# Order of the value projections and of the last products in the second mixer's head pairs

## The chip, the cores and the metric

The kernel runs on one core of a Trainium2 chip. The metric is the device time of one execution in microseconds. The kernel before took 2727.28 us (median of 3 runs, 2727.0 to 2727.28).

## The reference

One step of an encoder with two layers, 1024 channels, over a prompt of 1024 frames and 8 running streams of 16 frames each (1152 rows in all). Layer 0 mixes with stick-breaking attention and a convolution; layer 1, the one that the change touches, with attention in a band of chunks. After each mixer comes a residual and an MLP. The mixer of layer 1:

```
def c_project(h, w_in):
    p = (h @ w_in).reshape(B, T, 3, N_C_HEADS, HEAD_DIM)
    return p[:, :, 0], p[:, :, 1], p[:, :, 2]
...
def band_attention(q, k, v, q_pos, k_pos, rel_bias):
    s = jnp.einsum('bqhd,bkhd->bhqk', q, k).astype(jnp.float32) * (HEAD_DIM ** -0.5)
    rel = jnp.clip(q_pos[:, None] - k_pos[None, :], -REL_CLIP, REL_CLIP) + REL_CLIP
    s = s + rel_bias[:, rel].astype(jnp.float32)
    ...
    p = jax.nn.softmax(jnp.where(mask, s, -jnp.inf), axis=-1)
    return jnp.einsum('bhqk,bkhd->bqhd', p.astype(v.dtype), v)
...
o = lax.map(one_chunk, jnp.arange(T // CHUNK))
return o @ w_out, k[:, T - keep:], v[:, T - keep:]
```

It has 16 heads of 64 channels; a frame sees its chunk of 64 and the 8 chunks before. The new keys and values are outputs too.

## The kernel before

Channels lie on the 128 partitions and frames along the free axis, in three groups of 384. Every float32 operand of a matmul is split into a high and a low part (`split`: ACT copies the high part, L185, DVE subtracts it, L186), and each product is made of three matmuls.

The program is written as lists of steps. `Step(pe, go, dve, name, after, lag)` holds an estimated TensorE time, the code that issues the instructions, and optionally a name, and the name of a step that has to end some time (`lag`, ns) ahead. `merge` takes several such lists and makes one: of the heads that are ready on an estimated TensorE clock, it takes the one of the list that is least far along. `run` issues them. A scheduler then lays down each engine's queue; what an engine issues, it issues in that order.

The second mixer (`mixer1`) works on head pairs p = 0 to 7. A pair's work:

- **Projections.** Chunk 3p + n is q (n = 0), k (n = 1) or v (n = 2) of pair p: 72 matmuls `psc<-h,hl_wc` of 128 x 384, 24 for each of the three groups. A chunk's weights come in two halves `hl_wc{chunk}_0` and `_1`, loaded by SP into one of three staging buffers and split by ACT and DVE into one of four buffers; so the halves of a chunk go where those of the chunk two before it were. `staged` multiplies the sums by the row's norm (DVE, L1141) into `sq`, `sk` or `sv` and stores keys and values (POOL's DMA queue).
- **`expand_qk`.** For each of the two heads i, ACT copies k (L348) and q (L350), DVE makes the low parts l (L351) and q (L353), each 64 x 1024, and DMAs copy k and l to the other partitions.
- **`expand_v`.** TensorE turns the values (`vt`, L1169), and they are split into `vs`.
- **Jobs (i, t).** i is the head, t a quarter of the frames; each has two blocks q = 2t and 2t + 1 of 128 rows. `one(q)`: scores `zc` (L1220, L1221), bias and minimum on DVE (L1184, tile `s{p}{i}{q}`), exponential on ACT (L1187), reciprocal and scaling on DVE (L1188, L1189). Then `split_weigh_steps`: transposes of the weights in two or three groups gi (`tpc{p}{i}{t}{gi}`, L457), their parts `whc` (ACT) and `wlc` (DVE), the products `avc{p}{i}{t}` (L469), `atc` (ACT, L477), `cpc` (DVE, L479), and a DMA to `cat_d`. A job's transposes and products (its tail) are carried and woven into the next job by `pipeline`, and those of a pair's last job into the next pair.
- **Sample.** The running streams' attention of the pair (`zs`, `zn`, `st`, `so`, `sq`) is merged in.

All of this is merged per pair. Before the change, the fill of pair p was the three chunks of pair p + 1 (`proj(p + 1)`), with those of pair 0 issued ahead of the loop; the list of the pair's steps began with the carried ones, and `bias_p` and `expand_qk` were called just ahead of the merge.

Pair 7 has no pair to project for. Its fill is the output projection (`part_out`: `psoa<-cat,hl_wo1a`, added to `xo`, which is loaded from `x_d`, L1100, L1105), whose input `cat` comes from the pairs before: `ready_chunks` loads a pair's result (`cr<-cat_d`, L1081) and splits it into `cat`. `cr` uses the buffer of `sk`, `xo` those of `sq` and `sv`.

Of the kernel before, what the change touches and what calls it, by code (L numbers as in the profile page):

```python
# [22 lines left out]
NG = 3  # L23
# [29 lines left out]
def merge(*lists):  # L53


    lists = [steps for steps in lists if steps]
    total = [sum(s.pe for s in steps) or 1.0 for steps in lists]
    at, done = [0] * len(lists), [0.0] * len(lists)
    out, now = [], 0.0
    ends = {s.name: 1e9 for steps in lists for s in steps if s.name}  # L60
    while True:
        heads = []
        for n, steps in enumerate(lists):
            if at[n] < len(steps):
                s = steps[at[n]]
                ready = max(now, ends.get(s.after, -1e9) + s.lag)
                heads.append((ready, (done[n] + 0.5 * s.pe) / total[n], n, s))
        if not heads:
            return out
        now, _, n, s = min(heads, key=lambda e: e[:3])  # L70
        out.append(s)
        at[n] += 1
        done[n] += s.pe
        now += s.pe
        if s.name:
            ends[s.name] = now
# [22 lines left out]
def run(steps):  # L99
    for s in steps:  # L100
        s.go()
# [23 lines left out]
def tile_trunk(ctx, tc, ins, outs):  # L125
# [17 lines left out]
    def bank(name):  # L143
        return psum.tile([P, 512], F32, tag="ps", name=name)
# [165 lines left out]
    def chunk_steps(n, got, ahead, h, ks, evac, name, depth=1, per=12):  # L310

        steps = [Step(0.0, lambda: [ahead(n + d) for d in range(depth + 1)], 1200.0)]
        for g in range(NG):
            box = {}

            def ps(g=g, box=box):
                if "p" not in box:
                    box["p"] = bank(f"ps{name}{g}")
                return box["p"]

            steps += dense(ps, lambda: got[n], h, g, ks, per)
            steps.append(Step(0.0, lambda g=g, ps=ps: evac(ps(), g), 470.0))
        return steps

    def chunks_steps(ns, got, ahead, h, ks, evac, name, depth=1):

        steps = [Step(0.0, lambda: [ahead(n) for n in range(ns[0], ns[-1] + depth + 1)])]
        for g in range(NG):
            for n in ns:
                box = {}  # L330

                def ps(g=g, n=n, box=box):
                    if "p" not in box:
                        box["p"] = bank(f"ps{name}{n}{g}")
                    return box["p"]

                steps += dense(ps, lambda n=n: got[n], h, g, ks)
                steps.append(Step(0.0, lambda n=n, g=g, ps=ps: evac(n, ps(), g), 470.0))
        return steps
# [303 lines left out]

        return cs

    def pipeline(jobs, carry):


        steps = []
        for first, second, tail in jobs:  # L650
            h = (len(carry) + 1) // 2
            steps += [first] + carry[:h] + [second] + carry[h:]
            carry = tail
        return steps, carry

# [419 lines left out]
    def ready_chunks(layer, chunks, pp, cat_t):  # L1075

        steps = []
        for c in chunks:
            def go(c=c):
                cr = pp.tile([P, T], F32, "sk", f"cr{layer}{c}")  # L1080
                dma(cr, cat_d[layer][c])  # L1081
                for g in range(NG):
                    hi, lo = (x[:, c % 4, :] for x in cat_t[g][c // 4])
                    split(hi, lo, cr[:, g * G:g * G + G])
            steps.append(Step(300.0, go))
        return steps
# [29 lines left out]
    def mixer1(nx, win):  # L1116
        h, rstd = nx.h, nx.r
        with ExitStack() as st:
            ep = Bufs(st.enter_context(pool("early1")), s=4, bp=2)
            cp = Bufs(st.enter_context(pool("cache1")), ct=2)  # L1120
            pp = Bufs(st.enter_context(pool("pair1")))
# [6 lines left out]
            got, ahead = win  # L1128
            ks = range(KC)

            def staged(p, n, ps, g):
                tag = ("sq", "sk", "sv")[n]
                if p == 0 and n < 2:
                    if n == 0:
                        nx.run_rows(g)
                    elif g == 0:
                        nx.end(1)
                        nx.end(2)
                if g == 0:
                    S[tag, p] = pp.tile([P, T], F32, tag, f"{tag}1{p}")  # L1140
                tt(S[tag, p][:, g * G:g * G + G], ps[:, :G], rstd[g], ALU.mult)  # L1141
                if g == 2 and n:
                    put(outs["c_k" if n == 1 else "c_v"][p], S[tag, p])

            def proj(p):
                if p == 0:
                    return (chunks_steps([0, 1], got, ahead, h, ks, lambda n, ps, g: staged(0, n, ps, g), "c")
                            + [Step(0.0, lambda: expand_qk(0))]
                            + chunk_steps(2, got, ahead, h, ks, lambda ps, g: staged(0, 2, ps, g), "c02"))
                steps = []  # L1150
                for n in range(3):
                    steps += chunk_steps(3 * p + n, got, ahead, h, ks, lambda ps, g, n=n: staged(p, n, ps, g),
                                         f"c{p}{n}")
                return steps

            def expand_qk(p):
                q, k = S["sq", p], S["sk", p]
                expand(qs, kd, kl, q, k)
                S["qn"] = pp.tile([P, P], F32, "qn", f"qn1{p}")
                S["kn"] = pp.tile([P, P], F32, "kn", f"kn1{p}")  # L1160
                ACT(S["qn"], q[:, TP:], AF.Copy, scale=0.125)
                ACT(S["kn"], k[:, TP:], AF.Copy)

            def expand_v(p, g):
                v = S["sv", p]
                tp = bank(f"vt1{p}{g}")
                for i in range(3):
                    c = (3 * g + i) * P
                    nc.tensor.transpose(tp[:, i * P:(i + 1) * P], v[:, c:c + P], ident)  # L1169
                n = 3 if g < 2 else 2  # L1170
                tv = tp[:, :G].rearrange("p (j h d) -> p j h d", j=3, h=2)
                dst = vs[:, 3 * g:3 * g + n]
                split(dst[:, :, :, 0, :], dst[:, :, :, 1, :], tv[:, :n])
                if g == 2:
                    S["vn"] = pp.tile([P, P], F32, "vn", f"vn1{p}")
                    ACT(S["vn"], tp[:, 2 * P:3 * P], AF.Copy)
# [22 lines left out]
            def bias_p(p, i):  # L1199
                bp = ep.tile([P, 640], F32, "bp", f"bp{p}{i}")  # L1200
                dma(bp, ins["bias_p"][2 * p + i])
                nc.gpsimd.memset(bp[0:64, 576:640], NEG)
                nc.gpsimd.memset(bp[64:128, 0:64], NEG)
                S["bp", p, i] = bp
# [34 lines left out]
            def soft(bg, z, zn, s):  # L1239
# [3 lines left out]
                softmax(w, [(z[0], bs[:, 0:512], 0, 512), (zn[:, 0:P], bs[:, c:c + P], 512, P)], 640, f"s{p}{bg}")  # L1243
                s["w"] = w

            run(proj(0))
            carry, cat_t = [], None
            for p in range(8):
                S["p"] = p
                if p == 7:  # L1250
                    cat_t = new_hs("cat1")
                cat = Cat(1, p, wk, cat_t)
                jobs = attend(p, cat)
                s3 = jobs[3][0]
                s3.go = lambda p=p, go=s3.go: (bias_p(p, 1), go())
                body, left = pipeline(jobs[1:], jobs[0][2])
                steps = carry + [jobs[0][0]]
                steps += [Step(327.0, lambda p=p, g=g: expand_v(p, g)) for g in range(NG)]
                if p == 7:
                    bias_p(p, 0)  # L1260
                    expand_qk(p)
                    run(merge(steps, ready_chunks(1, range(3), pp, cat_t)))
                    steps = []
                steps += [jobs[0][1]] + body
                carry = left
                cs = sample_out(cat, wk, p)
                sample = [Step(0.0, lambda p=p: biases(p))]
                load = sample_caches(1, p, cp)
                sample += two_samples(*(sample_steps(1, p, bg, S, wk, load, soft, cs) for bg in range(2)))
                back = []  # L1270
                if p < 7:
                    fill = proj(p + 1)
                else:
                    fill = sum(part_out(1, range(3), pp, cat_t), [])
                    steps += carry
                    back = ready_chunks(1, range(3, 7), pp, cat_t)
                if p < 7:
                    bias_p(p, 0)
                    if p:
                        expand_qk(p)  # L1280
                run(merge(steps, sample, fill, back))
            return cat_t

# [527 lines left out]
    with pool("mlp0") as mp_:  # L1811
# [3 lines left out]
        early = []  # L1815
# [170 lines left out]
```

## Time and profile before

| | |
|---|---|
| median of 3 runs | 2727.28 us |
| profiled execution, its own time | 2730.68 us |
| its span in the trace | 2728.9 us |
| mean TensorE clock granted | 0.993 |
| second mixer's pair 3, from the sq of pair 2's end to that of its own | 70.2 us |
| window from the end of pair 6 to the end of pair 7's merge | 89.6 us |

So 1.8 us of the profiled execution lie around the span, and it took 3.4 us more than the median. In the page of the profile a group of instructions has a line, an engine, out<-in by the program's names, shapes and a count, then the busy time and the mean of one, then the idle time ahead of them and what ended most of it. In a timeline each row is a stretch of equal instructions with its start, length, and in brackets the idle ahead of it with its releaser. The largest groups of the second mixer's projections read:

```
L225 PE MATMUL psc<-h,hl_wc 128*128 128x384 f32 x1728 | 327.1, 339 | 0.0
L225 PEld LDWEIGHTS psc<-h,hl_wc 128*128 128x128 f32 x1728 | 296.8, 188 | 13.3 <-issue 10.9
```

### The profile page before, as it was taken

The numbers are of one execution on the slowest core, as the hardware profiler recorded it, in microseconds if no ns is written. First come the engines' busy times: TensorE is split into PE (matmuls) and PEld (weight loads), VectorE is DVE, ScalarE is ACT, GpSimd is POOL, SyncE is SP. The second block draws the span as 40 slices with busy tenths as digits, with TensorE's granted clock in tenths as the row PEclk, the third lists the DMA queues.
The fourth block names the chain that finished last, engine by engine and source line by source line (L and its number), as shares of the span: only waits on it lengthen the run. The fifth ranks groups of instructions, "written<-read, shape, count | busy, mean of one in ns | idle before, by whom it ended". The sixth has DMA issues, their size and how long they took to land.

```text
span 2728.9 us, 50505 instructions
## 1 busy us (share of the span) xinstructions
PE 2662.6 (98%) x19362; PEld 2553.8 (94%) x19362; DVE 2040.6 (75%) x4105; ACT 1365.7 (50%) x2854; POOL 330.5 (12%) x599
## 2 busy tenths in 40 slices
PE   8999998999999999999999999998999999999998
PEld 8888886899999999999999999997999999999998
DVE  7999996787777755768577777778787777647577
ACT  5344456755555543445355555555455555534344
POOL 1000111131111100000011111110321111100001
PEclk9999999999999999999999999999999999999999
DMA  4344447443333486335444444446543334674344
GB/s 159 104 128 149 146 141 241 171 145 141 140 138 138 151 290 224 108 113 178 145 141 139 129 139 141 137 127 218 181 140 138 143 141 147 233 254 135 96 125 146
DMA packets 173203, 422.90 MB, mean 155 GB/s; under 512 B 25968, under 2 KB 53808, under 8 KB 170912
## 3 DMA queue, kind: packets, MB, share of 16 engines
q1 hardware_dynamic: 135696, 288.38, 32.6%
q0 software_dynamic: 37120, 131.27, 13.9%
q8 instruction: 152, 2.49, 0.4%
q14 instruction: 91, 0.75, 0.1%
q10 hardware_dynamic: 144, 0.02, 0.0%
HBM read 289.60 MB, written 117.34 MB: 149 GB/s over the span
## 4 chain that ended last, share of the span: by engine, by line
PE 84%; DVE 7%; ACT 3%; issue 3%; DMA 3%; POOL 0%; SPq 0%; DVEq 0%; ACTq 0%; POOLq 0%
PE pd L1705 26%; PE um L1480 25%; PE psc L225 10%; PE psp L225 4%; PE avc L469 2%; PE tpc L457 2%; PE psoa L225 2%; PE f L225 1%; PE zs L570 1%; PE zc L1220 1%; PE ava L398 1%; DVE y L737 1%; PE so L604 1%; PE psg L225 1%; PE psa L225 1%
## 5 line engine op out<-in xcount | busy, mean ns | idle before, releaser
L225 PE MATMUL psc<-h,hl_wc 128*128 128x384 f32 x1728 | 327.1, 339 | 0.0
L225 PEld LDWEIGHTS psc<-h,hl_wc 128*128 128x128 f32 x1728 | 296.8, 188 | 13.3 <-issue 10.9
L1480 PE MATMUL um<-sl,hl_m 128*128 128x288 f32 x1548 | 240.8, 296 | 0.0
L1480 PEld LDWEIGHTS um<-sl,hl_m 128*128 128x128 f32 x1548 | 218.2, 189 | 0.0
L1705 PE MATMUL pd<-tm,hl_wd 128*128 128x288 f32 x1584 | 214.7, 294 | 0.0
L1705 PEld LDWEIGHTS pd<-tm,hl_wd 128*128 128x128 f32 x1584 | 211.3, 189 | 0.0
L737 DVE SCALAR_TENSOR_TENSOR y<-u,dw,y 128x1024 f32<-128x1024 f32 (+1 forms) x232 | 177.5, 805 | 0.7
L1487 ACT ACTIVATE hdm<-hdm 128x288 f32<-128x288 f32 x192 | 84.7, 442 | 156.4 <-DVE hdm L1486 154.8
L225 PE MATMUL psp<-h,hl_wi 128*128 128x384 f32 x864 | 162.5, 340 | 0.0
L186 DVE TENSOR_TENSOR tm<-xr,tm 128x576 fp32r<-128x576 f32 (+1 forms) x120 | 85.7, 715 | 94.8 <-ACT tm L185 94.6
L225 PEld LDWEIGHTS psp<-h,hl_wi 128*128 128x128 f32 x864 | 148.4, 188 | 6.2 <-issue 5.1
L185 ACT ACTIVATE tm<-xr 128x576 fp32r<-128x576 f32 (+1 forms) x120 | 77.6, 647 | 94.7 <-PE pd L1705 75.9
L1480 PE MATMUL um<-sl,hl 128*128 128x288 f32 x756 | 119.1, 296 | 0.0
L1187 ACT ACTIVATE s<-s,mxc 128x640 f32<-128x640 f32 (+4 forms) x128 | 88.8, 694 | 60.2 <-DVE mxc L1184 58.6
L1705 PE MATMUL pd<-th,hl_wd 128*128 128x288 f32 x792 | 113.9, 297 | 3.8 <-DVE th L186 3.7
L1705 PEld LDWEIGHTS pd<-th,hl_wd 128*128 128x128 f32 x792 | 108.7, 191 | 4.5 <-DVE th L186 4.2
L1705 PE MATMUL pd<-xr,hl_wd 128*128 128x288 f32 x792 | 111.9, 295 | 0.0
L1705 PEld LDWEIGHTS pd<-xr,hl_wd 128*128 128x128 f32 x792 | 107.4, 189 | 0.0
L1480 PEld LDWEIGHTS um<-sl,hl 128*128 128x128 f32 x756 | 106.4, 188 | 0.8
L1705 PE MATMUL pd<-tm,hl 128*128 128x288 f32 x768 | 104.9, 295 | 0.0
L1705 PEld LDWEIGHTS pd<-tm,hl 128*128 128x128 f32 x768 | 103.1, 188 | 0.0
L185 ACT ACTIVATE whc<-tpc 128x512 fp32r<-128x512 f32 (+1 forms) x144 | 72.5, 523 | 46.7 <-PE tpc L457 45.7
(530 smaller groups left out, 6536.8 us busy)
## 6 DMA issues: line engine op xcount, KB each, us to landing
xr<-hb_d SPq DMA_DIRECT2D x208, 288.0 KB, 2.9
xr<-in_w_up_dram SPq DMA_DIRECT2D x64, 512.0 KB, 4.0
hb_d<-hdm POOLq DMA_DIRECT2D x96, 288.0 KB, 2.4
hb_d<-t POOLq DMA_DIRECT2D x96, 288.0 KB, 2.4
wm<-in_w_down_dram SPq DMA_DIRECT2D x64, 256.0 KB, 4.1
st_wd<-in_w_down_dram SPq DMA_DIRECT2D x64, 256.0 KB, 3.5
st_wc<-in_w_in_c_dram SPq DMA_DIRECT2D x44, 256.0 KB, 2.6
xm_d<-xo POOLq DMA_DIRECT2D x16, 576.0 KB, 3.8
```

What stands on the lines that cost most here:

```text
L185: ACT(hi, src, AF.Copy)
L186: return tt(lo, src, f(hi), ALU.subtract)
L225: mm(ps()[:, :G], hl[:, a, at:at + P], act[g][k // 4][b][:, k % 4, :], start=n == 0, stop=n == len(todo) - 1)
L398: mm(st["av"][64 * m:64 * m + 64, o0:o0 + n], vs[:, j, i], st["w"][gi][:, c0:c0 + n], start=gi == 0, stop=gi == last)
L457: nc.tensor.transpose(tp[:, c0 + q * P:c0 + (q + 1) * P], blocks.get(j, tile_q), ident)
L469: mm(st["av"][:, o0:o0 + n], vs[:, j, i].rearrange("p a d -> p (a d)"), src[:, c0:c0 + n], start=st["done"] == 0, stop=st["done"] == nmm - 1)
L570: mm(box["z"][at // 512][own, at % 512:at % 512 + kw], qb[:, own], k[:, b * kw:b * kw + kw], start=True, stop=True)
L737: stt(src if j == CW - 1 else dst, src, wj, dst, ALU.mult, ALU.add)
L1187: ACT(s[:, :n], s[:, :n], AF.Exp, bias=mx, scale=-1.0, accum_out=tot)
L1480: mm(banks[b, n][:, :TQ], w[:, a, c * P:c * P + P], combo(key, c)[:, h, n * TQ:n * TQ + TQ], start=k < 3 and c == 0 and i == 0, stop=c == ...
L1487: ACT(y, y, AF.Relu)
L1705: mm(ps, w[:, a, m * P:m * P + P], b[:, h, (n - ns[0]) * TQ:(n - ns[0]) * TQ + TQ], start=first and s == 0, stop=j == NJ - 1 and s == 2, s ...
```

## The change

Two things are done in another order; no instruction of the program is removed or added. The values of pair p are projected in the merge of pair p itself, ahead of q and k of pair p + 1, and only q and k of pair 0 are issued ahead of the loop. And for pairs 0 to 6 `pipeline` stops ahead of the second half of the tail of the last job but one: that half and the last job's tail are carried to the next pair. `bias_p` and `expand_qk` become a step `x{p}` at the head of the pair's list, ahead of the carried steps; the first scores wait for it with a lag of 6000 ns, the values' transposes (`turned`) for the end of the value projection. In pair 7 the fill is the value projection, then `ready_chunks` of 0 to 2, then the output projection.

```
-    def pipeline(jobs, carry):
+    def pipeline(jobs, carry, over=False):
...
-            steps += [first] + carry[:h] + [second] + carry[h:]
+            steps += [first] + carry[:h] + [second]
+            if over and tail is jobs[-1][2]:
+                return steps, carry[h:] + tail
+            steps += carry[h:]
             carry = tail
...
-            def proj(p):
-                if p == 0:
...
-                for n in range(3):
+            def proj(p, *ns):
+                steps = []
+                for n in ns:
...
+                steps[-1].name = f"p{p}{ns[-1]}"
...
-            run(proj(0))
+            run(chunks_steps([0, 1], got, ahead, h, ks, lambda n, ps, g: staged(0, n, ps, g), "c"))
...
-                body, left = pipeline(jobs[1:], jobs[0][2])
-                steps = carry + [jobs[0][0]]
-                steps += [Step(327.0, lambda p=p, g=g: expand_v(p, g)) for g in range(NG)]
-                if p == 7:
-                    bias_p(p, 0)
-                    expand_qk(p)
-                    run(merge(steps, ready_chunks(1, range(3), pp, cat_t)))
-                    steps = []
-                steps += [jobs[0][1]] + body
+                body, left = pipeline(jobs[1:], jobs[0][2], p < 7)
+                jobs[0][0].after, jobs[0][0].lag = f"x{p}", 6000.0
+                turned = [Step(327.0, lambda p=p, g=g: expand_v(p, g)) for g in range(NG)]
+                turned[0].after, turned[0].lag = f"p{p}2", 1500.0
+                turned[-1].name = f"v{p}"
+                steps = ([Step(0.0, lambda p=p: (bias_p(p, 0), expand_qk(p)), 0.0, f"x{p}")] + carry
+                         + [*jobs[0][:2]] + turned + body)
...
-                back = []
+                sample[1].after, sample[1].lag = f"x{p}", 7000.0
+                fill, back = proj(p, 2), []
                 if p < 7:
-                    fill = proj(p + 1)
+                    fill += proj(p + 1, 0, 1)
                 else:
-                    fill = sum(part_out(1, range(3), pp, cat_t), [])
                     steps += carry
+                    early = ready_chunks(1, range(3), pp, cat_t)
+                    early[-1].name = "early"
+                    parts = sum(part_out(1, range(3), pp, cat_t), [])
+                    parts[0].after, parts[0].lag = f"v{p}", 0.0
+                    parts[1].after, parts[1].lag = "early", 4000.0
+                    fill += early + parts
                     back = ready_chunks(1, range(3, 7), pp, cat_t)
-                if p < 7:
-                    bias_p(p, 0)
-                    if p:
-                        expand_qk(p)
+                    back[0].after = "early"
                 run(merge(steps, sample, fill, back))
```

**The boundary of pairs 2 and 3.** TensorE's queue before, at the end of pair 2 (`psc322` is the third group of pair 3's values; job (1, 2) of pair 2 is `tpc212`, `avc212`):

```order
L1221 MATMUL zc216384_16953<-l1_14071,q1_14067 128x256
L225 MATMUL psc322_16922<-h1_40_13588,hl_wc11_1_16400 128x384
...
L225 MATMUL psc322_16922<-h1_70_13702,hl_wc11_1_16400 128x384
L457 MATMUL tpc2120_16976<-ident_69,s214_16874 128x128
L457 MATMUL tpc2120_16976<-ident_69,s215_16906 128x128
...
L612 MATMUL sq121_16994<-ident_69,sb121_16862 128x128
L469 MATMUL avc212_17001<-whc2120_16981,vs1_14072 128x256 x2
```

The same place now (`psc312` is the third group of pair 3's keys, `psc320` the first of its values):

```order
L225 MATMUL psc312_16775<-h1_70_13702,hl_wc10_1_16256 128x384
L469 MATMUL avc211_16857<-whc2110_16818,vs1_14072 128x256 x2
...
L1221 MATMUL zc216384_16875<-l1_14071,q1_14067 128x256
L612 MATMUL sq121_16886<-ident_69,sb121_16772 128x128
L457 MATMUL tpc2120_16893<-ident_69,s214_16798 128x128
...
L457 MATMUL tpc2120_16893<-ident_69,s215_16830 128x128
...
L469 MATMUL avc212_16911<-whc2120_16898,vs1_14072 128x256 x2
...
L225 MATMUL psc320_16978<-h1_00_13739,hl_wc11_0_16578 128x384
```

The twelve projection rows between `zc216` and `tpc212` are gone from there: the projections of the old merge end ahead of `avc211`, and those of the new one begin behind `avc212`.

ACT's queue at the same place, before (`hl_wc13_1` is the second weight half of chunk 13, the keys of pair 4):

```order
L1187 ACTIVATE s214_16874,totc214_16885<-s214_16874,mxc2141_16883 128x640
L185 ACTIVATE hl_wc13_0_17069<-st_wc13_0_17067 128x512
L1187 ACTIVATE s215_16906,totc215_16917<-s215_16906,mxc2151_16915 128x640
L477 ACTIVATE atc211_16944<-avc211_16935 64x256
L1187 ACTIVATE s216_16949,totc216_16960<-s216_16949,mxc2161_16958 128x640
L185 ACTIVATE hl_wc13_1_17074<-st_wc13_1_17072 128x512
L185 ACTIVATE whc2120_16981<-tpc2120_16976 128x512
L185 ACTIVATE whc2121_16990<-tpc2121_16985 128x512
L348 ACTIVATE k1_14069<-sk13_16540 64x1024
```

And now (`hl_wc12_1` is the second weight half of chunk 12, whose buffer held that of chunk 10, which `psc312` reads):

```order
L1187 ACTIVATE s214_16798,totc214_16809<-s214_16798,mxc2141_16807 128x640
L185 ACTIVATE hl_wc12_1_16964<-st_wc12_1_16962 128x512
L1187 ACTIVATE s215_16830,totc215_16841<-s215_16830,mxc2151_16839 128x640
L477 ACTIVATE atc211_16866<-avc211_16857 64x256
L348 ACTIVATE k0_14068<-sk13_16690 64x1024
L1162 ACTIVATE kn13_16948<-sk13_16690 128x128
L185 ACTIVATE whc2120_16898<-tpc2120_16893 128x512
L1187 ACTIVATE s216_16871,totc216_16882<-s216_16871,mxc2161_16880 128x640
L185 ACTIVATE whc2121_16907<-tpc2121_16902 128x512
L348 ACTIVATE k1_14069<-sk13_16690 64x1024
```

The second weight half stands ahead of the exponential of `s215` now, and `k0` of the new pair ahead of the first `whc212`.

DVE's queue there now, from the scaling of `s214` on (`sk13` is the last evacuation of pair 3's keys):

```order
L1189 TENSOR_SCALAR s214_16798<-s214_16798,totc214_16809 128x640
L1144 TENSOR_TENSOR sk13_16690<-psc312_16775,rh1_14036 128x384
L186 TENSOR_TENSOR hl_wc12_1_16964<-st_wc12_1_16962,hl_wc12_1_16964 128x512
L1188 RECIPROCAL totc215_16841<-totc215_16841 128x1
L479 TENSOR_TENSOR cpc211_16868<-avc211_16857,atc211_16866 64x256
L1189 TENSOR_SCALAR s215_16830<-s215_16830,totc215_16841 128x640
```

Before, the weight's low half there was that of `hl_wc13_0`, ahead of the reciprocal of `s215`, and the evacuation (`sv13`) stood behind `cpc211`.

**Pair 7.** TensorE's queue at the end of pair 6 before (`tpc613` is pair 6's last job, `vt170` the first transposes of pair 7's values):

```order
L469 MATMUL avc612_20611<-whc6121_20600,vs1_14072 128x256 x2
L457 MATMUL tpc6130_20671<-ident_69,s616_20559 128x128
...
L469 MATMUL avc612_20611<-wlc6122_20635,vs1_14072 128x128 x2
L457 MATMUL tpc6130_20671<-ident_69,s617_20616 128x128
...
L1220 MATMUL zc7000_20745<-k0_14068,q0_14066 128x128
...
L1169 MATMUL vt170_20754<-ident_69,sv17_20390 128x128
```

The same place now (`psc720` is the first group of pair 7's values):

```order
L469 MATMUL avc612_20531<-whc6121_20527,vs1_14072 128x256 x2
L225 MATMUL psc720_20588<-h1_00_13739,hl_wc23_0_20198 128x384
...
L469 MATMUL avc612_20531<-whc6122_20580,vs1_14072 128x128 x2
L457 MATMUL tpc6130_20622<-ident_69,s616_20491 128x128
L457 MATMUL tpc6130_20622<-ident_69,s617_20536 128x128
...
L469 MATMUL avc612_20531<-wlc6122_20581,vs1_14072 128x128 x2
L225 MATMUL psc721_20642<-h1_00_13739,hl_wc23_0_20198 128x384
```

The 24 matmuls of `psc720` lie between the products of job (1, 2) and the last job's transposes, and those of `psc721` behind them. SP's queue of loads for pair 7, before:

```order
L1100 DMA xo11_20835<-x_d_111 128x1152
L541 DMA ct17v00_21052<-in_band_v_dram 128x2048
L1081 DMA cr12_20709<-cat_d1_110 128x1152
L1081 DMA cr13_20884<-cat_d1_110 128x1152
L1100 DMA xo12_20877<-x_d_111 128x1152
L1081 DMA cr14_21141<-cat_d1_110 128x1152
```

And now:

```order
L541 DMA ct17v00_20805<-in_band_v_dram 128x2048
L192 DMA st_wo1a5_0_21333<-in_w_out_c_dram 128x384
L541 DMA ct17v10_21220<-in_band_v_dram 128x2048
L1084 DMA cr12_20784<-cat_d1_110 128x1152
L1103 DMA xo11_20973<-x_d_111 128x1152
L192 DMA st_wo1a6_0_21443<-in_w_out_c_dram 128x384
L1084 DMA cr13_20794<-cat_d1_110 128x1152
L1084 DMA cr14_20869<-cat_d1_110 128x1152
L1103 DMA xo12_20988<-x_d_111 128x1152
```

Both loads of the sample's cached values (`ct17v`) come ahead of `cr12`, and the third `xo` behind `cr13` and `cr14`.

More of the change, by code (lines that the diff above doesn't have):

```diff
@@ L1143, in staged @@
                     put(outs["c_k" if n == 1 else "c_v"][p], S[tag, p])
-            def proj(p):
-                if p == 0:
-                    return (chunks_steps([0, 1], got, ahead, h, ks, lambda n, ps, g: staged(0, n, ps, g), "c")
-                            + [Step(0.0, lambda: expand_qk(0))]
-                            + chunk_steps(2, got, ahead, h, ks, lambda ps, g: staged(0, 2, ps, g), "c02"))
+            def proj(p, *ns):
                 steps = []
-                for n in range(3):
+                for n in ns:
                     steps += chunk_steps(3 * p + n, got, ahead, h, ks, lambda ps, g, n=n: staged(p, n, ps, g),
                                          f"c{p}{n}")
+                steps[-1].name = f"p{p}{ns[-1]}"
                 return steps
```

## The prediction

> **What bounds the kernel now.** I read the busy times and the chain first, then the waits of TensorE in the second mixer (1300 to 1930 us), then windows cut at the head pairs.
>
> ```profile
> PE 2662.6 (98%) x19362; PEld 2553.8 (94%) x19362; DVE 2040.6 (75%) x4105; ACT 1365.7 (50%) x2854; POOL 330.5 (12%) x599
> PE 84%; DVE 7%; ACT 3%; issue 3%; DMA 3%; POOL 0%; SPq 0%; DVEq 0%; ACTq 0%; POOLq 0%
> ```
>
> TensorE (PE) is busy for 98% of the span and holds 84% of the chain that ended last. The same instructions run before and after the change, so the sum of their times cannot move; only PE's waits, and PE's clock, can. The waits of the second mixer:
>
> ```profile
> PE avc L469 <- ACT whc L185: 6.9, 7, 1.1
> PE tpc L457 <- DVE s L1189: 6.1, 8, 3.2
> PE psoa L225 <- DVE cpc L479: 2.1, 2, 1.9
> PE avc L469 <- DVE wlc L186: 2.1, 2, 1.5
> ```
>
> The columns are us in total, times, longest. These four rows hold 17.2 us, under 1% of the kernel. By windows, one row for a middle pair and one for the last (busy us and instructions of PE, weight loads, DVE, ACT, POOL; then PE's clock, DMA share, GB/s):
>
> ```profile
> 1485.00:1555.10 70.10, 68.54 (x507) 64.55 (x506) 51.77 (x145) 38.00 (x89) 9.06 (x21) 1.00 0.45 137
> 1835.60:1925.20 89.60, 79.23 (x548) 71.47 (x547) 72.47 (x205) 51.89 (x126) 7.34 (x15) 0.96 0.60 203
> ```
>
> A middle pair leaves PE 1.6 us without work in 70.1; the last stretch, from the end of pair 6 through pair 7, leaves 10.4 in 89.6. So the largest sum to be had lies in pair 7, and what the change could spoil is in the 70 us pairs, which hardly wait.
>
> **The boundary of two pairs, before.** The waits sit where one pair hands over to the next. PE at the boundary of pairs 2 and 3 (start, length, ... , idle before and its releaser), and the first boundary's only wait:
>
> ```profile
> 1420.57 0.55 PE L457 MATMUL tpc<-ident,s 128*128 128x128 f32 x3 [0.69 <-DVE s L1189]
> ...
> 1554.24 1.04 PE L457 MATMUL tpc<-ident,s 128*128 128x128 f32 x8
> 1555.11 0.27 PE L612 MATMUL sq<-ident,sb 128*128 128x128 f32 x1
> 1556.53 0.51 PE L469 MATMUL avc<-whc,vs 128*128 128x256 f32 x2 [1.15 <-ACT whc L185]
> ...
> 1561.39 0.77 PE L225 MATMUL psc<-h,hl_wc 128*128 128x384 f32 x3
> 1562.54 0.88 PE L457 MATMUL tpc<-ident,s 128*128 128x128 f32 x6 [0.38 <-DVE s L1189]
> ```
>
> Eight 128-wide transposes start 0.87 us apart from the next row, 0.11 each. From sq to avc are 1.42 us, less 0.11 for sq: 1.31 lost. From the three psc rows to tpc are 1.15 us, less 3 x 0.2: 0.55 lost (starts against starts give about 0.16 more than the idle column, which ends a matmul late). A regular boundary thus costs 1.86 us. Five of them (1-2 to 5-6) and the first (0.69 + 0.16 = 0.85) make **10.2 us**.
>
> The seventh, from pair 6 to pair 7, has no projections to fill it:
>
> ```profile
> 1836.77 0.50 PE L469 MATMUL avc<-whc,vs 128*128 128x256 f32 x2 [0.90 <-ACT whc L185]
> 1839.30 0.44 PE L469 MATMUL avc<-whc,vs 128*128 128x128 f32 x2 [0.28 <-ACT whc L185]
> 1843.44 1.54 PE L457 MATMUL tpc<-ident,s 128*128 128x128 f32 x6 [3.25 <-DVE s L1189]
> ```
> ```profile
> 1554.00:1558.00 4.00, 2.85 (x23) 2.58 (x22) 3.49 (x10) 2.98 (x6) 1.66 (x3) 1.00 0.46 172
> ...
> 1839.90:1843.40 3.50, 0.30 (x2) 0.15 (x2) 3.36 (x6) 1.73 (x4) 0.94 (x3) 0.77 0.90 227
> 1843.40:1849.00 5.60, 5.45 (x26) 5.05 (x27) 3.17 (x6) 2.57 (x6) 0.76 (x3) 0.54 1.01 271
> 1884.00:1888.00 4.00, 2.10 (x15) 1.60 (x13) 3.44 (x11) 1.35 (x4) 0.00 (x0) 1.00 0.74 290
> ```
>
> It waits 4.43 us (0.48 more by starts), and after the long wait PE works 5.6 us at a clock of 0.54, which costs 5.6 x 0.46 = 2.6. Together **7.5 us**.
>
> **What the change does there.** It removes and adds no instruction. In all seven boundaries, 0-1 to 6-7, the order becomes one pattern: the last projection rows of the next pair's k end *ahead* of the second half of the pair's last half job but one, and until the value projections of the next pair begin PE has only attention rows of the old pair. At the first six this takes away cover: before, twelve rows of psc stood between zc and tpc. At 6-7 it adds cover, since the 72 matmuls of pair 7's values (72 x 0.18 = 13 us) are interleaved there now. I follow PE from P0, the issue of the last psc row of k, with the lengths of the same operations before:
>
> ```profile
> 1550.84 0.63 ACT L185 ACTIVATE hl_wc<-st_wc 128x512 fp32r<-128x512 f32 x1 [1.08 <-PE psc L225]
> 1551.37 0.82 ACT L1187 ACTIVATE s<-s,mxc 128x640 f32<-128x640 f32 x1
> ...
> 1557.54 1.05 ACT L348 ACTIVATE k<-sk 64x1024 fp32r<-64x1024 f32 x1 [0.58 <-PE zc L1220]
> ```
> ```profile
> 1550.89 0.55 DVE L1189 TENSOR_SCALAR s<-s,totc 128x640 f32<-128x640 f32 x1
> 1551.50 0.69 DVE L186 TENSOR_TENSOR hl_wc<-st_wc,hl_wc 128x512 fp32r<-128x512 f32 x1
> 1552.31 0.16 DVE L1188 RECIPROCAL totc<-totc 128x1 f32<-128x1 f32 x1
> ...
> 1553.43 0.42 DVE L479 TENSOR_TENSOR cpc<-avc,atc 64x256 f32<-64x256 f32 x1
> ...
> 1554.44 0.56 DVE L1141 TENSOR_TENSOR sv<-psc,rh 128x384 f32<-128x384 f32 x1
> ...
> 1559.68 1.22 DVE L351 TENSOR_TENSOR l<-sk,k 64x1024 fp32r<-64x1024 f32 x1
> ...
> 1562.51 1.22 DVE L353 SCALAR_TENSOR_TENSOR q<-sq,q 64x1024 fp32r<-64x1024 f32 x1
> ```
>
> (a) ACT's copy of the second weight half (hl_wc..1) needs that last psc row, since it overwrites the weights which that row reads; the first row shows ACT waiting so already (1.08 us), only where nothing stood behind. Now the exponential of the pair's tile s..5 stands behind it: 0.2 (the matmul's own end) + 0.63 + 0.82 = 1.65. On DVE the scaling of s..4 (0.55), the evacuation of k (0.56), the low half of the weight (0.69), the reciprocal (0.16), cpc (0.42) and the scaling of s..5 (0.55) stand in this order, so s..5 is ready at about 0.5 + 0.56 + 0.69 + 0.16 + 0.42 + 0.55, with hand-overs of some 0.6: 3.5 us after P0. PE has until then the products avc of the job before (0.89), zc (0.63), sq and two transposes (0.33), which are estimates from the steps of these kinds in the same timeline and end at 1.85. **Lost 1.65**; 1.28 if the scaling of s..4 is done before P0, 2.2 if one more DVE row of 0.55 is late.
>
> (b) Then the first avc waits for ACT's whc of the new transposes, behind k0 (1.05 us), as it does now: 0.6 taken, between 0 and the 1.31 of before.
>
> (c) DVE now has l0, l1 and q1 (3 x 1.22 = 3.7 us) together ahead of the scaling of s..7, where before one of them stood. Fifteen DVE rows of these lengths (8.2 us) lie from the scaling of s..5 to the end of that of s..7: 3.5 + 8.2 and some 0.7 of waiting for whc make 12.4 us after P0. PE, from its avc at 4.8, has 27 psc rows (4.9) and some 2.1 us of attention: 11.8. Lost 0.6, between 0 and 1.22.
>
> So a boundary after costs 1.65 + 0.6 + 0.6 = **2.85 us**, bounds 1.28 and 4.7. Seven cost 20 us against 10.2 + 7.5 = 17.7: **+2.3**.
>
> **Pair 7 behind its boundary.** Four waits stand there, and two of the DMAs that let them come:
>
> ```profile
> 1885.26 0.47 PE L469 MATMUL avc<-whc,vs 128*128 128x256 f32 x2 [0.37 <-DVE xo L1105]
> 1887.28 0.50 PE L469 MATMUL avc<-wlc,vs 128*128 128x256 f32 x2 [1.54 <-DVE wlc L186]
> 1901.25 1.32 PE L225 MATMUL psoa<-cat,hl_wo1a 128*128 128x384 f32 x6 [1.89 <-DVE cpc L479]
> 1905.85 0.45 PE L469 MATMUL avc<-wlc,vs 128*128 128x256 f32 x2 [0.56 <-DVE wlc L186]
> ```
> ```profile
> 1884.56 0.55 DVE L1105 TENSOR_TENSOR xo<-xo,psoa 128x384 f32<-128x384 f32 x1 [3.60 <-DMA xo<-x_d]
> ```
> ```profile
> 1899.82 0.52 ACT L185 ACTIVATE cat<-cr 128x384 fp32r<-128x384 f32 x1 [3.21 <-DMA cr<-cat_d]
> ```
>
> They sum to 4.36, 5.0 by starts: two engine stalls on a load, of 3.60 and 3.21 us, of which some 2 us each come through to PE. After, three places can stall so. The transposes of v wait for DVE's last evacuation of values, behind a piece of cr1's low half; a wlc stands behind three pieces of cr4; and the third xo load now stands behind cr3 and cr4 on SP's queue. Three such at 2 us make 6: **+1.0**, between -5.0 (none comes through) and +5.0 (they come through twice as far). The rest of the pairs keeps its cover: the fill is still 216 psc rows a pair. At the start, the first attention has two chunks instead of three behind it; what is lost is under 1 us and counted at nothing, because the value projections of pair 0 (13 us) run there at once.
>
> **Sum.** +2.3 + 1.0 = +3.3 us. The profiled execution took 2730.68 us (span 2728.9) and so would take 2734.0; the runs shown have a median of 2727.28, 3.4 less, from which I predict **2730.5**.
>
> **Rivals.** *Faster.* The new pattern costs no more than the old one: DVE is through with its rows at P0, whc comes in time, and (c) vanishes, so that a boundary costs the 1.86 of before and the seventh loses its 7.5. 7 x 1.86 - 17.7 = -4.7, and with one stall in pair 7 fewer (-2): 2720.6, and down to 2716 with a clean pair 7. For it: pair 7's gap is really filled, and a middle pair's DVE is busy for 51.8 of 70.1 us only. Against it: the rows are in order, and the weight's copy truly waits for P0.
>
> *Slower.* The place is ACT's hl_wc..1 at P0, with s..5's exponential behind it, and DVE's low half and cpc behind that. If one DVE row more (0.55) is late and (b) is at its old 1.31, a boundary costs 2.2 + 1.31 + 0.6 = 4.1; halfway to it, 3.5, gives 24.5 - 17.7 + 1.0 = +7.8: 2735. It decides from 5.5 = 7b - 17.7 + 1.0, b = 3.2 us a boundary.
>
> *The clock.* Around P0 PE now works about 1.9 us and waits 1.65, and again 0.6. The windows show the clock dropping only in the wait of 3.25 us (0.77, then 0.54), and at 1.00 where PE was busy 2.1 of 4 us. If it drops all the same, each boundary loses the 2.6 us once more: 7 x 2.6 + 3.3 = +21.5: 2749. By the row of 1884 to 1888, half busy at full clock, I give it 0.04. [...]
>
> *No effect.* The order of the engines' rows moves as described, so that the change does nothing can only mean that all of this cancels; that lies within the forecast.
>
> **How the numbers follow.** Forecast (a boundary of 2.3 to 3.2 us, pair 7 within 3 us of before) 0.55; faster 0.16; slower by the late exponential 0.25; the clock 0.04. The range takes the forecast, most of the faster case and the slower one: boundaries of 1.9 with a better pair 7 give 2720, boundaries of 3.4 with a worse pair 7 (+3) 2736; I let it end at 2738. Within 0.2% (5.5 us, about what a measurement of this kernel can tell from no change) lie the forecast and the near edges of the two cases beside it: same 0.56, faster 0.15, slower 0.29.
>
> **What would show it.** Right: at each boundary tpc with an idle of 1.1 to 1.5 us behind DVE's s, a clock of 1.00 at 6-7, and pairs of 71 us instead of 70.1. Step (a) is wrong if the tpc behind sq shows no wait; (b), if avc behind ACT's whc is above 1 us; (c), if the last tpc of the boundary follows without a wait. The forecast is wrong if pair 7 waits for a load by 4 us or more at one place, or if middle pairs show new waits between the boundaries.

## The result, and the profile after

| | before | changed |
|---|---|---|
| median, us (12 runs each) | 2727.14 (2723.31 to 2731.47) | 2732.22 (2727.35 to 2740.49) |
| ratio of the times, 95% interval | | 1.0023 (1.0015 to 1.0031) |
| profiled execution: its own time, span, mean clock | 2730.68, 2728.9, 0.993 | 2740.49, 2738.7, 0.989 |
| second mixer, from the start of its first psc to that of its last sq | 613.48 | 621.18 |

The kernel became slower by 0.23%, 6 us by the ratio. The profiled execution of the changed kernel is the longest of its twelve runs, so its trace shows more of the loss than a usual run has. Of the 9.8 us between the two spans, 7.7 lie in the second mixer. The first psc starts 1.3 us later (1311.21 against 1312.50), with nothing changed ahead of it: over the traces below that start lies anywhere from 1305.5 to 1312.5 us, so I compare the mixer's own stretch.

TensorE's waits in the second mixer of the changed kernel (us in total, times, longest):

```profile
PE tpc L457 <- DVE s L1189: 10.4, 7, 1.6
PE avc L469 <- ACT whc L185: 3.1, 8, 0.4
PE psoa L225 <- DVE wlc L186: 2.3, 1, 2.3
PE psoa L225 <- ACT cat L185: 1.6, 1, 1.6
PE tpc L457 <- DVE xo L1108: 1.1, 1, 1.1
...
PE zc L1221 <- DMA l<-l: 1.0, 1, 1.0
```

Before, four rows held 17.2 us; these hold 19.5. That is not the loss. The boundary of pairs 2 and 3 on TensorE:

```profile
1548.98 0.27 PE L612 MATMUL sq<-ident,sb 128*128 128x128 f32 x1
1549.09 0.38 PE L457 MATMUL tpc<-ident,s 128*128 128x128 f32 x2
1551.07 0.88 PE L457 MATMUL tpc<-ident,s 128*128 128x128 f32 x6 [1.59 <-DVE s L1189]
1552.36 0.79 PE L469 MATMUL avc<-whc,vs 128*128 128x256 f32 x2 [0.42 <-ACT whc L185]
1552.95 0.52 PE L1220 MATMUL zc<-k,q 128*128 128x384 f32 x1
```

The two waits are there as the steps (a) and (b) had them. New is the last row: a zc of 128 x 384 took 0.34 us at the same place before, 0.52 here. Windows say why (the number behind POOL's count is TensorE's clock):

```profile
1549.00:1551.00 2.00, 0.48 (x5) 0.24 (x3) 1.94 (x6) 1.95 (x5) 0.83 (x2) 1.00 0.24 68
1551.00:1555.60 4.60, 4.11 (x19) 3.88 (x20) 3.70 (x13) 3.46 (x7) 1.60 (x4) 0.63 0.76 247
...
1837.10:1841.70 4.60, 4.13 (x28) 3.90 (x29) 4.32 (x14) 4.27 (x8) 2.16 (x4) 1.00 0.82 258
```

Behind the wait the clock is 0.63 over 4.6 us; 4.6 x 0.37 / 0.5 = 3.4 us of it ran at half. The last row is a stretch of the same length behind the boundary of pairs 6 and 7, where the first wait was 0.88 us: full clock, and 28 rows done instead of 19 (in part other ones, since the values' projection runs there). A middle pair and the last stretch:

```profile
1548.98:1620.69 71.71, 69.70 (x507) 66.00 (x506) 51.19 (x146) 38.22 (x89) 9.20 (x21) 0.98 0.43 134
1835.80:1933.90 98.10, 90.25 (x622) 83.28 (x621) 78.76 (x216) 54.02 (x129) 9.68 (x19) 0.98 0.62 202
```

The pair took 71.7 us where it took 70.1, and PE was *busier* in it (69.7 against 68.5 us) with the same rows: slow rows count as busy. In the last stretch, from the end of pair 6 through pair 7, 7.9 us are left without work instead of 10.4, though it holds some 75 rows more.

### The profile page after: what moved, and what is told of

It reads as the page before. It is cut to its first block, busy times and chain, and to the rows that moved or that the text cites. A ratio compares the mean times of both kernels' runs of the same rounds, so it can differ in the third digit from the quotient of the medians.

```text
span 2738.7 us, 50469 instructions
## 1 busy us (share of the span) xinstructions
PE 2671.2 (98%) x19362; PEld 2564.0 (94%) x19362; DVE 2038.0 (74%) x4105; ACT 1366.3 (50%) x2854; POOL 330.6 (12%) x599
## 4 chain that ended last, share of the span: by engine, by line
PE 70%; DVE 5%; DMA 2%; ACT 1%; issue 1%; DVEq 0%; ACTq 0%; SPq 0%; POOLq 0%
PE pd L1706 26%; PE um L1481 25%; PE psc L225 10%; PE avc L469 2%; PE tpc L457 2%; PE psoa L225 1%; PE zc L1220 1%; PE zc L1221 1%; DMA cr<-cat_d 1%; PE so L604 1%; PE zs L570 1%; PE psob L225 0%; DVE s L1184 0%; DVE xr L1387 0%; DVE wlc L186 0%
## 5 line engine op out<-in xcount | busy, mean ns | idle before, releaser
L185 ACT ACTIVATE whc<-tpc 128x512 fp32r<-128x512 f32 (+1 forms) x144 | 73.1, 524 | 90.3 <-PE tpc L457 88.7
```

What stands on the lines that cost most here:

```text
L185: ACT(hi, src, AF.Copy)
```

## Experiments

All ratios are to the kernel before, run on the same chip beside it. The mixer column is the stretch from the first psc to the last sq in the profiled execution.

| run | ratio (95% interval) | mixer, us | pairs, us |
|---|---|---|---|
| before | 1 | 613.5 | 70.1 |
| changed | 1.0023 (1.0015 to 1.0031) | 621.2 | 71.7 |
| changed, second profile | 1.0019 (1.0010 to 1.0028) | 619.8 | 70.8 and 71.7 |
| values moved only | 1.0061 (1.0046 to 1.0076) | 628.0 | 72.5 and 73.1 |
| half carried only | 1.0043 (1.0026 to 1.0060) | 621.1 | 71.8 |
| 14 transposes added | 1.0032 (1.0020 to 1.0044) | 620.6 | 71.6 |
| low part on GpSimd | 1.0023 (1.0013 to 1.0032) | 619.2 | 70.7 |
| the same, not at the start | 1.0004 (0.9995 to 1.0014) | 614.7 | 70.7 |
| first value rows left at the pair's end | **0.9975 (0.9966 to 0.9984)** | 607.1 | 69.9 |

**The changed kernel again**, for the clock.

> The changed kernel once more, for a second profile. If half clock behind the wait is what varies from run to run, a run that takes about 2732 us shows the same waits of 1.59 and 0.42 us at six boundaries, but half clock at fewer of them, and its pairs are 71.7 us where the clock drops and 70.6 us where it does not. If the slow rows belong to the order, all pairs take 71.7 us in any run.

This profiled execution has both cases side by side. First the boundary of pairs 1 and 2, then that of 2 and 3:

```profile
1474.25 0.88 PE L457 MATMUL tpc<-ident,s 128*128 128x128 f32 x6 [1.59 <-DVE s L1189]
1475.55 0.50 PE L469 MATMUL avc<-whc,vs 128*128 128x256 f32 x2 [0.42 <-ACT whc L185]
1475.89 0.34 PE L1220 MATMUL zc<-k,q 128*128 128x384 f32 x1
...
1483.01 0.55 PE L457 MATMUL tpc<-ident,s 128*128 128x128 f32 x3 [0.26 <-DVE s L1189]
...
1545.06 0.88 PE L457 MATMUL tpc<-ident,s 128*128 128x128 f32 x6 [1.59 <-DVE s L1189]
1546.35 0.79 PE L469 MATMUL avc<-whc,vs 128*128 128x256 f32 x2 [0.42 <-ACT whc L185]
1546.94 0.52 PE L1220 MATMUL zc<-k,q 128*128 128x384 f32 x1
```
```profile
1471.27:1474.68 3.41, 1.82 (x16) 1.59 (x15) 3.35 (x11) 2.77 (x6) 1.33 (x3) 1.00 0.28 76
1474.68:1478.09 3.41, 2.99 (x23) 2.75 (x21) 3.08 (x9) 3.17 (x6) 0.88 (x2) 1.00 0.88 292
1542.95:1546.36 3.41, 1.40 (x12) 0.93 (x10) 3.25 (x12) 2.66 (x7) 1.63 (x3) 1.00 0.52 163
1546.36:1549.77 3.41, 3.41 (x14) 3.41 (x15) 2.61 (x6) 2.96 (x5) 0.96 (x2) 0.50 0.63 210
...
1472.18:1542.97 70.79, 68.52 (x507) 64.51 (x506) 51.20 (x146) 38.18 (x89) 9.01 (x21) 1.00 0.44 136
1542.97:1614.76 71.79, 69.78 (x507) 66.09 (x506) 51.19 (x146) 38.19 (x89) 9.18 (x21) 0.98 0.44 134
```

The same program, the same waits to 0.01 us; the clock dropped at one and not at the other, and the pair behind the drop took 1.0 us more. It dropped at four of the six boundaries here (0.63 over the 4.6 us behind each, 1.00 behind the other two), at all six in the first profile. So the slow rows are the clock's, not the order's, and this may be one reason why the runs of the changed kernel lie 13 us apart: the two longest of the twelve, 2740.5 and 2739.0 us, have the lowest mean clocks, 0.989 and 0.988.

What set the two boundaries apart can be read from the times of the drops. They start at 1546.36, 1618.04, 1689.72 and 1761.40 us here, 71.68 apart, and each lasts 3.41 us. In the first profile they start at 1408.84, 1480.52, 1552.20, 1623.88, 1695.56 and 1767.24, again 71.68 apart, which is 21 times 3.4133. In that profile and in the one of the kernel before, the 22 half-clock stretches that end within the kernel last 3.41 or 6.83 us, and within a profile all of them start a whole number of times 3.4133 us from each other, to 0.01 us. So the clock's changes in an execution all lay on one grid with a spacing of 3.41 us (its points are called ticks below), and where it lay differed from one execution to another. The windows above are cut at the ticks. Ahead of the drop, both waits of the boundary fell between two ticks, and PE was busy for 1.40 of 3.41 us; at the boundary without a drop a tick parted them (at 1474.68), and the emptier window still held 1.82 us of work. The kernels with waits of 1.59 and 0.42 us (this one twice, and the two of the next paragraph) have 23 such boundaries: the 18 with a drop had 1.4 to 1.6 us of work in the window ahead of it, the five without had 1.8 us or more in each window there. Elsewhere in the kernel the line is not as clean: the first profile has drops behind 2.11 and 2.24 us of work (at 436.04 and 599.88 us), the profile of the kernel before has none behind 1.99 and 1.95 (the windows from 950.89 and 1899.80 us). So PE's busy time between two ticks alone did not tell whether the clock dropped.

It also shows why the drops came in a row here: a pair with a drop lasted 71.7 us, almost exactly 21 ticks, so the next boundary met the ticks at nearly the same place and dropped too. A pair without one lasted 70.8 us, 0.9 less, and moved on against the ticks; the second profile had two such pairs before the first drop.

**Each part alone.** The two parts were taken apart: once without the carried half, once without the moved values.

```
-                body, left = pipeline(jobs[1:], jobs[0][2], p < 7)
+                body, left = pipeline(jobs[1:], jobs[0][2])
```

> Only the moved value projections are left; the last half job's products stay in their own pair. If the boundary's cost comes from the value projections (no projection rows between the scores of s..6 and the first products), the transposes wait 1.6 us and the products 0.4 us at six boundaries as in the changed kernel, the pairs take 71.7 us and the time is 1.001 to 1.003 of before. If it comes from the carried half, the waits fall below 0.5 us, a pair takes 70.1 us and the time is at or under that of before (0.998 to 1.000).

```
 (the kernel before, with the changed pipeline)
-                body, left = pipeline(jobs[1:], jobs[0][2])
+                body, left = pipeline(jobs[1:], jobs[0][2], p < 7)
```

> Only the carried half is left; values are projected a pair ahead as before. If the carried half makes the boundary (the projections of the merge end ahead of the products), the same waits of 1.6 and 0.4 us stand at the boundaries and pair 7 keeps its unfilled stretch (7.5 us): 1.002 to 1.005 of before, the slowest of this set. If only the moved values do it, the boundaries cost 1.86 us as before and the time is within 0.1% of before.

Either part alone makes the boundary: waits of 1.59 and 0.42 us at six boundaries with the values moved alone, at five (all but the first) with the half carried alone. With the values moved alone there are 19 waits of tpc for DVE instead of 7, 19.0 us in all, so its time is above what I expected (1.0061 against 1.003 at most): the carried half helps the moved values. The clock dropped behind three of its six boundaries (0.63 over the 4.6 us behind that of pairs 2 and 3). Two of these drops cost 0.6 us each (pairs of 73.1 instead of 72.5), the third nothing (72.6). At undropped boundaries TensorE waits another 1.37 us for DVE right behind, and at the three that wait was 0.60, so part of what the half clock took was probably lost anyway; why one cost less than the others isn't shown. The half alone came out in the range that I gave, but I had expected it to be the slowest of the set. Its clock dropped behind all five of its boundaries (0.64 and 0.63 over the 4.6 us behind two of them); its profiled execution was the fastest of four (2730.77 us, median 2736.57), so its mixer column flatters it.

**Work in the wait.** Fourteen repeats of the first transpose, into the same place, ahead of the transposes that wait:

```
+            if gi == 0 and cat.layer == 1 and cat.p < 7 and (i, t) == (1, 2):
+                j, c0, n = items[0]
+                for _ in range(14):
+                    nc.tensor.transpose(tp[:, c0:c0 + P], blocks.get(j, blocks.keys[j][0]), ident)
```

> The changed kernel with 14 transposes more at each of seven boundaries, which repeat the first one into the same place while TensorE would wait (14 x 0.11 = 1.5 us of work that changes nothing). If the clock is what costs (half clock for 3.4 us behind the wait), the granted clock stays 1.00 at the boundaries and a pair takes 70.5 to 70.8 us instead of 71.7, though 98 matmuls are added; time 2 to 7 us under the changed kernel. If the slow rows behind the wait come of how kinds of matmuls alternate there, the pair stays at 71.7 us or longer and the rows keep their lengths.

The boundary of pairs 2 and 3 on TensorE, and the pair's window:

```profile
1541.66 1.69 PE L458 MATMUL tpc<-ident,s 128*128 128x128 f32 x14
1543.19 0.27 PE L461 MATMUL tpc<-ident,s 128*128 128x128 f32 x1
1543.63 0.98 PE L461 MATMUL tpc<-ident,s 128*128 128x128 f32 x7 [0.17 <-DVE s L1193]
1546.21 0.50 PE L473 MATMUL avc<-whc,vs 128*128 128x256 f32 x2 [1.59 <-ACT whc L185]
1546.55 0.34 PE L1224 MATMUL zc<-k,q 128*128 128x384 f32 x1
```
```profile
1541.55:1613.18 71.63, 69.87 (x522) 66.12 (x521) 51.24 (x146) 38.21 (x89) 8.92 (x21) 1.00 0.44 134
```

Half of it came: the clock stays 1.00 over the whole pair, the wait for s..5 is filled, and zc is back at 0.34 us. But a wait of 1.59 us stands at the next product now, because in this kernel ACT's queue has the exponential of s..6, which waits 1.03 us for DVE, ahead of the whc that the product needs (in the changed kernel it stands behind). What the clock gave back, that wait and 1.5 us of added transposes took: no gain, where I had expected 2 to 7 us.

**DVE's rows ahead of s..5.** In the changed kernel, on ACT and on DVE behind the last projection of k:

```profile
1547.66 0.63 ACT L185 ACTIVATE hl_wc<-st_wc 128x512 fp32r<-128x512 f32 x1 [0.51 <-PE psc L225]
1548.41 0.83 ACT L1187 ACTIVATE s<-s,mxc 128x640 f32<-128x640 f32 x1
```
```profile
1548.29 0.55 DVE L1189 TENSOR_SCALAR s<-s,totc 128x640 f32<-128x640 f32 x1
1548.76 0.55 DVE L1144 TENSOR_TENSOR sk<-psc,rh 128x384 f32<-128x384 f32 x1
1549.22 0.68 DVE L186 TENSOR_TENSOR hl_wc<-st_wc,hl_wc 128x512 fp32r<-128x512 f32 x1
1549.82 0.15 DVE L1188 RECIPROCAL totc<-totc 128x1 f32<-128x1 f32 x1
1550.01 0.42 DVE L479 TENSOR_TENSOR cpc<-avc,atc 64x256 f32<-64x256 f32 x1
1550.46 0.55 DVE L1189 TENSOR_SCALAR s<-s,totc 128x640 f32<-128x640 f32 x1
```

DVE goes from row to row without an idle time of 0.1 us from 1548.29 to the scaling's end at 1551.0, where the transposes start. One of its rows was moved to GpSimd:

```
+        if name[:2] == "wc" and name[-2:] == "_1" and int(name[2:-2]) % 3 == 0 and name != "wc0_1":
+            ACT(hl[:, 0, :n], st[:, :n], AF.Copy)
+            nc.gpsimd.tensor_tensor(hl[:, 1, :n], st[:, :n], f(hl[:, 0, :n]), op=ALU.subtract)
+            return hl
```

> The changed kernel with the low part of the second weight half at each boundary subtracted on GpSimd instead of DVE. If DVE's row of rows sets the wait, the scaling of s..5 comes 0.4 to 0.6 us sooner, the wait falls from 1.59 to about 1.1 us, the clock stays 1.00 as at the boundary of pairs 6 and 7 (0.88 and 0.42 us of waiting), and a pair takes 70.1 to 70.6 us: 0.998 to 1.000 of before. If ACT's copy of that half with the exponential behind it sets it, the wait stays at 1.6 us and the clock drops as now.

```profile
1544.85 0.87 PE L461 MATMUL tpc<-ident,s 128*128 128x128 f32 x6 [1.04 <-DVE s L1193]
1546.14 0.51 PE L473 MATMUL avc<-whc,vs 128*128 128x256 f32 x2 [0.42 <-ACT whc L185]
...
1554.15 0.44 PE L473 MATMUL avc<-wlc,vs 128*128 128x128 f32 x2 [0.72 <-DVE wlc L186]
```
```profile
1472.64:1543.32 70.68, 68.51 (x507) 64.61 (x506) 50.55 (x145) 38.09 (x89) 10.51 (x23) 1.00 0.44 136
```

The boundary did as expected: 1.04 us instead of 1.59, a clock of 1.00, pairs 1.0 us shorter. Step (a) is a chain on DVE, and ACT's copy is no part of what sets it: the exponential behind the copy ends at 1549.24, 0.6 us before DVE comes to the reciprocal that needs it (1549.82). Nearly all of the 1.0 us is the clock's, though: the undropped pairs of the changed kernel took 70.8 us, and of the 0.55 us less of waiting only 0.1 shows in the pair, since avc now waits 0.72 us for a wlc, where those pairs waited 0.26 at step (c). The total did not follow, as the start of the mixer lost 3.4 us: there the same subtraction on GpSimd's queue came ahead of the DMAs that copy k, TensorE's first scores waited 2.0 us for k and 0.8 for l (1.0 for l alone in the changed kernel). The waits make 1.8 of the 3.4 us. Leaving that one half alone:

> The kernel with the low part on GpSimd, without doing so for the first such half, whose subtraction stood ahead of the DMAs that copy k and l at the start (TensorE waited 2.0 and 0.8 us for them). If that is where its gain went, the start comes back by 3 us, pairs stay at 70.7 us: 1.0005 to 1.0015 of before. If not, the same 1.0023.

It gave 614.7 us and 1.0004: about the time of before. The start came back as expected (92.9 us to the first boundary's sq instead of 96.3), the pairs stayed at 70.7, and the ratio is a little under the range that I gave. So the changed order at full clock is about level with the one before, and what it loses in the changed kernel is about what six drops cost (0.0019 of 2727 us is 5.2, six times 0.9 is 5.4).

**Rows that can run there.** The last run leaves the first 12 of the 72 value matmuls in the merge of the pair before, so that a projection is half done at the boundary:

```
-                fill, back = proj(p, 2), []
+                fill, back = rest, []
                 if p < 7:
-                    fill += proj(p + 1, 0, 1)
+                    rest = proj(p + 1, 2)
+                    fill = fill + proj(p + 1, 0, 1) + rest[:2]
+                    rest = rest[2:]
```

> The changed kernel, but the first 12 of the 72 matmuls of a pair's values are left at the end of the pair before, so that projection rows (12 there, and the next 12 right behind) stand where TensorE waits. If the lack of independent rows at that place is the cause of both the waits and the half clock, the waits of 1.59 and 0.42 us go, the clock stays 1.00, and a pair takes 68.3 to 69.2 us (71.7 less 2.3 of waiting and 1.1 of clock, with small ones left); with pair 7 as in the changed kernel that is 0.995 to 0.998 of before. If the wait only moves to the next product (as with the added transposes), a pair stays above 70.5 us and the time at or above that of before.

```profile
1540.96 0.42 PE L225 MATMUL psc<-h,hl_wc 128*128 128x384 f32 x1
1542.02 0.41 PE L457 MATMUL tpc<-ident,s 128*128 128x128 f32 x2 [0.64 <-DVE s L1189]
1542.19 1.66 PE L225 MATMUL psc<-h,hl_wc 128*128 128x384 f32 x8
1543.68 0.83 PE L457 MATMUL tpc<-ident,s 128*128 128x128 f32 x6
1544.27 0.77 PE L225 MATMUL psc<-h,hl_wc 128*128 128x384 f32 x3
1545.62 0.50 PE L469 MATMUL avc<-whc,vs 128*128 128x256 f32 x2 [0.57 <-ACT whc L185]
```
```profile
1540.93:1611.17 70.24, 68.94 (x507) 64.55 (x506) 51.74 (x146) 38.03 (x89) 8.93 (x21) 1.00 0.45 137
...
1820.60:1914.50 93.90, 88.83 (x610) 81.03 (x608) 76.48 (x214) 53.01 (x129) 8.39 (x17) 0.96 0.61 199
```

Twelve projection rows stand where TensorE waited, and the wait for s..5 is gone. A smaller one came ahead of it, 0.64 us for s..4 (0.28 at most other boundaries), and 0.57 for whc is left, so the pairs are at 69.7 to 70.2 us, not at 68.3 to 69.2: the pairs are only as good as before the change. The clock was 1.00 behind all six boundaries. The time is where I expected it, 0.9975, and below both kernels: with the pairs no longer worse, what is left is the filled stretch of pair 7, here 5.1 us without work instead of 10.4. So independent rows at this place took the waits of 2.0 us down to between 0.5 and 1.2 and held the clock at 1.00, but did not do away with them; why the pairs gained less than that over the 70.8 us of full clock isn't shown by a single row.

## Why the prediction came out as it did

The forecast was 2730.5 us in a range of 2720 to 2738; the median is 2732.2. The sum was +3.3 us; the medians lie 5.1 apart, the mixers of the two profiled executions 7.7. The direction and the waits were right; that the number came so close is in part luck, as two errors below work against each other (the clock left out, boundaries reckoned too dear), and the range reached to 2738 for the sake of a late exponential, not of the clock.

- **Step (a), 1.65 us.** Measured 1.76 (from the end of the second transpose, 1549.09 + 2 x 0.11, to 1551.07); its idle of 1.59 is a little over the 1.1 to 1.5 named as the sign. The DVE rows and their order were as worked out. Their end came 3.7 us after the issue of the last psc row, at 1547.29, instead of 3.5, and TensorE was through with its own rows after 2.0 instead of 1.85. That ACT's copy was part of the chain was wrong and cost nothing.
- **Step (b), 0.6.** Measured 0.42 of idle, 0.6 by starts.
- **Step (c), 0.6.** Measured 0.26 of idle, 0.4 by starts, where the clock held, and nothing where it dropped: there TensorE came later. By these rows a boundary at full clock costs 2.8 us, against 2.85 predicted. The pairs say less: 70.8 us instead of 70.1, so 0.65 more, where 2.85 - 1.86 = 0.99 was reckoned.
- **The boundary of pairs 6 and 7**, 7.5 us before, 2.85 predicted: 0.88 + 0.42 + 0.73 of idle, 2.6 by starts, at full clock.
- **Pair 7 behind it, +1.0.** Three stalls were named, and three came, one of them as named (2.35 us behind a wlc, which stood on DVE behind three pieces of a cr's low half). The transposes of v did not wait; instead psoa waited 1.57 us for ACT, which had waited 2.68 us for a cr:

```profile
1870.45 3.62 PE L225 MATMUL psoa<-cat,hl_wo1a 128*128 128x384 f32 x15 [1.57 <-ACT cat L185]
1879.23 0.66 PE L457 MATMUL tpc<-ident,s 128*128 128x128 f32 x4 [1.07 <-DVE xo L1108]
1885.54 1.33 PE L225 MATMUL psoa<-cat,hl_wo1a 128*128 128x384 f32 x6 [2.35 <-DVE wlc L186]
```
```profile
1869.88 1.35 ACT L185 ACTIVATE cat<-cr 128x384 fp32r<-128x384 f32 x3 [2.68 <-DMA cr<-cat_d]
```

  They make 5.0 us against the 4.36 of before, 0.6 more instead of 1.0. The clock dropped behind the last of them too (0.65 from 1885.5 to 1889.5).
- **The start, counted at nothing**, lost 1.0 us: the first zc waits for the DMA that copies l.
- **The clock: the step that failed.** The rival was written down with its place, but at a chance of 0.04 and 2.6 us a boundary. It came at four to six of seven boundaries, at about 0.9 to 1.0 us. Six times 0.9 make 5.4 us, and with the 1.0 of the start 6.4, more than the 4.4 by which the first profile's mixer is over the sum; the 2.0 between them is about what six boundaries at full clock came cheaper than reckoned (6 x 0.34, an estimate from the pairs). I had dismissed the clock by one window, 1884 to 1888, half busy at 1.00, and by the drop in a wait of 3.25 us. The first was cut across a tick of the clock: by the ticks of that trace, which are at 1882.72, 1886.14 and 1889.55, PE was busy for 2.65 and 2.27 of 3.41 us there. And the other drop did not need the whole wait: it starts at 1841.77, halfway through it, behind a window with 1.53 us of work, as much as a boundary of the changed kernel leaves. Its price came from that longer drop, two ticks long (6.8 us) instead of one; here the half clock lasts 3.4 us, and the wait of step (c) behind it, 0.26 us at full clock, was not there where the clock had dropped.

No stretch of 3.41 us was idle at these boundaries: the longest wait there was 1.59 us, and the clock dropped behind 1.4 to 1.6 us of work between two ticks.

So the forecast of a small loss rests on the right waits, and its size was short by the clock.

## What to carry to other kernels

When work is moved to another stage, look at what independent rows it leaves at the place that it came from: a dozen matmuls that waited for nothing, kept at the hand-over, shortened the waits here (2.0 us to between 0.5 and 1.2) and held the clock at 1.00 as well (pairs of 69.9 us instead of 71.7). Where a trace has slow rows right behind a wait, read the granted clock of a window cut there before looking for a cause in the order; busy time alone hid it here (69.8 of 71.8 us with the drop, 68.5 of 70.8 without). If the same place drops in one execution and not in another, look at when the drops start before calling it chance. And a wait that is filled may reappear at the next instruction, as the 1.59 us did here behind the added transposes, so an added filler is judged by the period of the whole stage.

## What the hardware showed that I had not expected

- In the profiles of the kernel before and of the changed one, the clock changed only at ticks 3.41 us apart, which lay elsewhere in another execution. Waits of 1.59 and 0.42 us halved it until the next tick (3.41 us at 0.50) where they left 1.4 to 1.6 us of work between two ticks, and did not where a tick parted them so that 1.8 us or more were left on each side: six of six boundaries in one execution, four of six in another of the same program. With 1.04 and 0.42 us the clock stayed at 1.00 behind all twelve boundaries of the two kernels with the low part on GpSimd.
- A pair with a drop lasted 71.7 us, 21 ticks, so the next boundary met them at nearly the same place: once one had dropped, all later ones up to that of pairs 5 and 6 did, in both profiles of the changed kernel and in the one with the half alone.
- A drop cost about 0.9 us of 70.8, not the 1.7 that 3.4 us at half clock would make if TensorE alone set the pace, and between nothing and 0.6 where TensorE waited for DVE right behind it.
- One row of 128 x 512 on GpSimd's queue ahead of two copies cost the start of the mixer 3.4 us: 1.8 of it in TensorE's waits for k and l (2.0 and 0.8 us, against 1.0 for l alone).
